# RWKV-7 and differential attention, one layer: dense products among the second head pair's transposes

## The chip, the cores and the metric

The kernel runs on one core of a Trainium2 chip. Five engines work beside each other, each on its own list of instructions: TensorE (matmuls, into PSUM), VectorE (DVE), ScalarE (ACT), GpSimd (POOL) and SyncE (SP, which issues most DMAs). The metric is the device time of one execution in microseconds (us), the median of several runs.

## The reference, cut to what matters

One decoder layer on 512 prompt tokens and 8 x 8 sample tokens, 576 columns in all, with a model width of 1024. Everything is float32.

```python
def layer_forward(x, prev_row, S0, attend, lam_init, lp):
    xn = rmsnorm(x, lp['g_mix'], NORM_EPS)
    P = xn @ lp['w_in']                        # RWKV columns, q k v, two gates
    ...
    Pr = Pr + (Pprev - Pr) * lp['mu_shift']    # token shift
    o_a, S = rwkv7_branch(Pr, S0, lp)          # 8 heads of 64, a recurrence over tokens
    ...
    att = attend(q, k, v, lam)                 # differential attention with ALiBi
    m = gate_a * (o_a @ lp['w_br_a']) + gate_b * (o_b @ lp['w_br_b'])
    x = x + m @ lp['w_out']
    hn = rmsnorm(x, lp['g_ffn'], NORM_EPS)
    x = x + jnp.square(jax.nn.relu(hn @ lp['w_up'])) @ lp['w_down']

def rwkv7_scan(S0, r, w, k, v, a, b):
    def step(S, inp):
        r_t, w_t, k_t, v_t, a_t, b_t = inp
        sa = jnp.einsum('bhij,bhj->bhi', S, a_t)
        S = S * w_t[:, :, None, :] + sa[..., None] * b_t[:, :, None, :] + v_t[..., None] * k_t[:, :, None, :]
        return S, jnp.einsum('bhij,bhj->bhi', S, r_t)
```

## The kernel before, in words

Activations lie transposed in SBUF, channels on the 128 partitions and 576 tokens along the free axis. Each weight matrix is streamed in blocks of 128 output channels. A block's weights are split in a high and a low half, and each 128 x 288 result is built from three products per 128 input channels: high by high, high by low, low by high. These are the **dense products**: `ps_z` (the RWKV projections, `shifted`), `ps_g` (the gates, `gate`), `ps_brb` and `ps_bra` (the two branch outputs), and later `ps_wo`, `u...` and `ps_dn` (output projection and MLP).

`stream` (a generator) yields before every product. Generators stand in a list, `waiting`. `take(n)` issues the next n products of that list at this place of the program; `fill(n)` does the same, and queues each of them behind the last matmul that the program has issued so far (`ring["mm"]`, set by the helpers `mm` and `tr`), by an edge that only fixes the order on TensorE. A planner turns the program into one order for each engine: of what it holds ready it takes what stands first in the program. So a taken product may be moved forward into any time in which it thinks that TensorE waits; a filled one not beyond its matmul. Each product adds to the bank of the one before, so products leave the list strictly in order. The kernel uses eight banks of PSUM: two for the dense products, three ("psw") that `bank` hands out in turn for most other work, three for the inverse and the chain.

The RWKV branch works on four **head pairs** (hp 0 to 3, two heads of 64 on 128 partitions). `rwkv(hp)` is a generator of stages, and `run(...)` advances it by one stage per number:

- A: key norms (`pn`), decay and rate (`pw`, `pa`), normalised keys (`pk`), bonus (`pbn`), then the masked 128 x 128 score blocks of nine chunks of tokens (`pA`), which VectorE masks out of PSUM into `ABR` and `ST`. Two groups of 8 products are asked for, behind pn and behind pa.
- B: token-major transposes of v (`pV`, five, evacuated by ScalarE into `SVU`) and of the keys (`pK`, nine, into `KBt`), the DMA of the sample states `s0`, and their products (`pI`).
- C: a triangular inverse by doubling (`pW`, `pZ`, eight blocks in turn, each with 9 products tied behind it, after one product by itself), ending in `TT`.
- D: new sample states (`pF`). E: mean and variance. F: transposes back (`pTy`), gate (`pg`), and the output `oa`, for hp 2 and 3 split into the halves `oab` that `ps_bra` reads.

`chain(pr)` is the recurrence over nine chunks for two head pairs at once (`pch`, `pY`).

The order is written out by hand at the end of this part of the kernel (lines 1051 to 1081): stages and numbers of products in turn. What the change touches: `run(0, 1, 1)` ran stage C of hp 0 and A and B of hp 1; `take(106)` came behind them, and `run(1)` was stage C of hp 1. In B of hp 1 eight products were asked for, with `take`, behind pK.

Of the kernel before, what the change touches and what calls it, by code (L numbers as in the profile page):

```python
# [41 lines left out]
def tile_hybrid_step(ctx, tc, xT, xsT, ktab, vtab, s0T, ptab, w_in, vecs, w2a2, g2, lamv,  # L42
# [14 lines left out]
    def act(out, in_, func=AF.Copy, **kw):  # L57
        ring["act"] = AE.activation(out=out, in_=in_, func=func, **kw)  # L58
# [9 lines left out]
    def ts(out, a, s1, op0, s2=None, op1=ALU.bypass, eng=None):  # L68
        (eng or VE).tensor_scalar(out=out, in0=a, scalar1=s1, scalar2=s2, op0=op0, op1=op1)

    def mm(out, lhsT, rhs, start=True, stop=True):
        ring["mm"] = PE.matmul(out=out, lhsT=lhsT, rhs=rhs, start=start, stop=stop)  # L72
        return ring["mm"]
# [27 lines left out]
    def bank(name):  # L101
        return psw.tile([P, 512], F32, tag="w", name=name)
# [113 lines left out]
    def take(n):  # L216

        while waiting and n:
            if next(waiting[0], None) is None:
                waiting.pop(0)  # L220
            else:
                n -= 1

    def fill(n):

        with tc.issue_after(ring["mm"].ins):
            take(n)
# [514 lines left out]
    def rwkv(hp):  # L742
# [11 lines left out]
        pn = bank(f"pn{hp}")  # L754
        for t, o in enumerate(toks):
            mm(pn[:, 2 * t:2 * t + 2], sq[:, o:o + P], c[:, C_HS:C_HS + 2])
        (fill if hp != 2 else take)(8)
        nr = stat.tile([P, 10], F32, tag="nr", name=f"nr{hp}")
        ts(nr, pn[:, 0:10], 1e-24, MAX)
        GE.tensor_tensor(out=nr, in0=nr, in1=mhalf[:, :10], op=ALU.pow)  # L760
# [6 lines left out]
        for t0, n in HALF:  # L767
# [3 lines left out]
            pa = bank(f"pa{hp}{t0}")  # L771
            mm(pa[:, :n], al[:, hs], Pt[12][:, t0:t0 + n])
            act(aa[:, t0:t0 + n], pa[:, :n], AF.Tanh, scale=0.5, bias=hw0[:, 4 + hp:5 + hp])
        (fill if hp != 2 else take)(8)
        ts(u, u, 1.0, ADD)
        cum = tmp("cum")
        VE.tensor_tensor_scan(out=cum, data0=reset, data1=u, initial=0.0, op0=MUL, op1=ADD)
# [65 lines left out]
        for cs, pV in two_chunks(f"pV{hp}", vv):  # L843
            for a, c0, c1 in cs:
                src = pV[64 * a:64 * a + 64].rearrange("p (c w) -> p c w", w=P)[:, :(c1 - c0 + 1) // 2]
                act(SVU[64:128, c0:c1:2, 0], src[:, :, 0:64])
                act(SVU[0:64, c0:c1:2, 1], src[:, :, 64:128])
        if hp >= 2:
            fill(8)
        KBt = rb_.tile([P, NCH, 2, 64], F32, tag="KBt", name=f"KBt{hp}")  # L850
        for c0, cn in ((0, 4), (4, 4), (8, 1)):
# [5 lines left out]

        s0 = rt.tile([P, NB, 64], F32, tag="s0", name=f"s0_{hp}")
        nc.sync.dma_start(out=s0, in_=s0T[hp])
        (fill if hp == 3 else take)(8)  # L860
        pI = bank(f"pI{hp}")
        for b in range(NB):
            for par, rows in halves:
# [177 lines left out]


    gens = [rwkv(hp) for hp in range(4)]

    def run(*stages):
        for hp in stages:
            while Pt[8 + hp] is None:
                take(2)
            next(gens[hp], None)
# [3 lines left out]
    waiting += ga[:5]  # L1053
    run(0, 0)
    take(221)
    run(0, 1, 1)
    take(106)
    run(1)
    chain(0)
    run(2, 0, 1)  # L1060
    take(190)
# [422 lines left out]
```

## Time and profile before

| | us |
|---|---|
| median of 3 runs | 1004.05 |
| lowest, highest | 1003.92, 1005.98 |
| the profiled execution | 1006.88 |
| its span, first to last instruction | 1005.1 |
| TensorE busy in it | 975.1 (97%) |
| VectorE busy | 688.9 (69%) |
| ScalarE busy | 497.0 (49%) |
| GpSimd busy | 87.5 (9%) |

A table by stretches gives busy time of each engine between two times from the span's start, and TensorE's granted clock as a share of full speed (1.00 is 2.4 GHz, 0.50 is 1.2 GHz). A timeline lists instructions in order of time; equal ones in a row are merged into one line. The number in brackets is idle time of the engine just before, and what ended it. "PE" is TensorE.

### The profile page before, as it was taken

Reading aid. Unit: us, or ns where it says so; the run is one execution under the profiler, and the core shown is the slowest. Engines: PE = TensorE matmul, PEld = TensorE weight load, DVE = VectorE, ACT = ScalarE, POOL = GpSimd, SP = SyncE. Lnnn points to the kernel's source line nnn. Section 1 sums busy time; section 2 is a strip of 40 time slices with the busy share of each in tenths; the row PEclk is TensorE's granted clock in tenths of the full one; section 3 lists DMA queues with packets and bytes.
Section 4 is the critical chain, followed back from the end, with each engine's and each line's share of the span. In section 5 each row is a group of like instructions: output and inputs, shape, how many; then the busy total and the mean of one; then the engine's idle time right before and its main releaser. Section 6 shows DMA issues by size and latency. Waiting matters only on the chain.

```text
span 1005.1 us, 24415 instructions
## 1 busy us (share of the span) xinstructions
PE 975.1 (97%) x10012; PEld 919.4 (91%) x10012; DVE 688.9 (69%) x1459; ACT 497.0 (49%) x1094; POOL 87.5 (9%) x171
## 2 busy tenths in 40 slices
PE   9999999899999998999989999999999999999996
PEld 9999998898887887988779999999999999999996
DVE  6698566864946679444579898966666666666644
ACT  6576455354435355453334666644444444444732
POOL 2511001301010340000210000000000000000001
PEclk9999999999989999999999999999999999999999
DMA  7422673211111234323357642222222222221402
GB/s 266 136 70 83 205 223 114 61 64 45 43 59 45 69 106 152 104 81 113 103 182 225 206 140 86 83 95 85 88 92 85 85 84 85 84 87 41 135 3 95
DMA packets 50833, 105.75 MB, mean 105 GB/s; under 512 B 6066, under 2 KB 8114, under 8 KB 50594
## 3 DMA queue, kind: packets, MB, share of 16 engines
q1 hardware_dynamic: 47442, 96.95, 30.4%
q0 software_dynamic: 1648, 5.35, 1.5%
q8 instruction: 79, 1.29, 0.5%
q10 hardware_dynamic: 1632, 1.89, 0.5%
q14 instruction: 32, 0.26, 0.1%
HBM read 89.38 MB, written 14.78 MB: 104 GB/s over the span
## 4 chain that ended last, share of the span: by engine, by line
PE 83%; DVE 6%; ACT 4%; issue 3%; DMA 2%; POOL 1%; SPq 0%; DVEq 0%; ACTq 0%; POOLq 0%
PE ps_dn L72 20%; PE ps_g L72 8%; PE ps_z L72 8%; PE ua L1220 5%; PE ux L1220 5%; PE ps_wo L72 4%; PE ps_k L72 3%; PE uc L1220 3%; PE ub L1220 3%; PE ud L1220 2%; PE ps_bra L72 2%; PE ps_q L72 2%; PE pch L72 2%; PE ps_brb L72 2%; PE ps_v L72 2%
## 5 line engine op out<-in xcount | busy, mean ns | idle before, releaser
L72 PE MATMUL ps_dn<-q,hi_dn 128*128 128x288 f32 x768 | 154.7, 296 | 0.0
L72 PEld LDWEIGHTS ps_dn<-q,hi_dn 128*128 128x128 f32 x768 | 122.7, 188 | 1.4
L72 PE MATMUL ps_dn<-q,lo_dn 128*128 128x288 f32 x384 | 113.2, 295 | 0.0
L72 PE MATMUL ps_g<-xl,hi_g 128*128 128x288 f32 x256 | 79.7, 311 | 0.0
L72 PE MATMUL ps_g<-xh,hi_g 128*128 128x288 f32 x256 | 79.0, 309 | 0.0
L72 PE MATMUL ps_g<-xh,lo_g 128*128 128x288 f32 x256 | 79.0, 309 | 0.0
L72 PEld LDWEIGHTS ps_dn<-q,lo_dn 128*128 128x128 f32 x384 | 72.0, 188 | 0.0
L72 PE MATMUL ps_z<-xh,lo_z 128*128 128x288 f32 (+1 forms) x224 | 68.9, 308 | 0.0
L72 PE MATMUL ps_z<-xh,hi_z 128*128 128x288 f32 (+1 forms) x224 | 67.6, 302 | 0.0
L72 PE MATMUL ps_z<-xl,hi_z 128*128 128x288 f32 (+1 forms) x224 | 66.8, 298 | 0.0
L61 DVE TENSOR_TENSOR ya<-ya,ps_dn 128x288 f32<-128x288 f32 x96 | 43.2, 451 | 29.4 <-PE ps_dn L72 29.4
L58 ACT ACTIVATE hi_dn<-raw_dn 128x512 fp32r<-128x512 f32 x48 | 30.1, 628 | 57.0 <-PE ps_dn L72 57.0
L1220 PE MATMUL ua<-h_b,hi 128*128 128x288 f32 x256 | 53.2, 298 | 0.0
L1220 PE MATMUL ux<-h_t,hi 128*128 128x288 f32 x256 | 52.3, 296 | 0.0
L58 ACT ACTIVATE c<-c 128x288 f32<-128x288 f32 x112 | 48.4, 439 | 7.4 <-DVE c L61 5.8
L72 PEld LDWEIGHTS ps_g<-xh,hi_g 128*128 128x128 f32 x256 | 48.7, 190 | 3.1 <-issue 1.8
L72 PEld LDWEIGHTS ps_g<-xl,hi_g 128*128 128x128 f32 x256 | 48.6, 190 | 1.9
L72 PEld LDWEIGHTS ps_g<-xh,lo_g 128*128 128x128 f32 x256 | 48.6, 190 | 1.6 <-DVE lo_g L61 0.2
L58 ACT ACTIVATE hi<-a 128x1024 fp32r<-128x1024 f32 (+1 forms) x32 | 27.1, 846 | 42.0 <-PE ps_dn L72 34.2
L72 PE MATMUL ps_dn<-q,w 128*128 128x320 f32 (+1 forms) x336 | 46.3, 297 | 0.0
L61 DVE TENSOR_TENSOR lo<-s,hi 128x1024 fp32r<-128x1024 f32 x32 | 39.2, 1224 | 10.1 <-ACT hi L58 10.0
L72 PEld LDWEIGHTS ps_dn<-q,w 128*128 128x128 f32 x336 | 45.3, 190 | 0.1
(395 smaller groups left out, 2802.2 us busy)
## 6 DMA issues: line engine op xcount, KB each, us to landing
a<-in_w_up_dram SPq DMA_DIRECT2D x32, 512.0 KB, 3.4
raw_dn<-in_w_down_dram SPq DMA_DIRECT2D x64, 256.0 KB, 2.8
raw_g<-in_w_in_dram SPq DMA_DIRECT2D x32, 256.0 KB, 3.1
raw_z<-in_w_in_dram SPq DMA_DIRECT2D x28, 256.0 KB, 3.1
gt_d<-gg SPq DMA_DIRECT2D x16, 288.0 KB, 2.4
g<-gt_d SPq DMA_DIRECT2D x16, 288.0 KB, 3.6
kp<-in_ktab_dram SPq DMA_DIRECT2D x16, 256.0 KB, 4.5
vp<-in_vtab_dram SPq DMA_DIRECT2D x16, 256.0 KB, 3.8
```

The lines of the kernel that those rows point to most:

```text
L58: ring["act"] = AE.activation(out=out, in_=in_, func=func, **kw)
L61: ins = (eng or VE).tensor_tensor(out=out, in0=a, in1=b, op=op)
L72: ring["mm"] = PE.matmul(out=out, lhsT=lhsT, rhs=rhs, start=start, stop=stop)
L1220: ring["mm"] = PE.matmul(out=ps[:, :288], lhsT=l[:, k], rhs=hb[blk][:, h, k], start=start and i == 0, stop=i == 11, skip_group_check=skip)
```

## The change

Stage B of hp 1 is now run behind the 106 products, directly ahead of its stage C. In that stage 8 products are asked for behind pV, which were not asked for before, and the 8 behind pK are now filled where they were taken. In stage A of hp 2 the two groups of 8 are filled where they were taken.

```diff
-        (fill if hp != 2 else take)(8)
+        fill(8)
         nr = stat.tile([P, 10], F32, tag="nr", name=f"nr{hp}")
...
-        (fill if hp != 2 else take)(8)
+        fill(8)
         ts(u, u, 1.0, ADD)
...
-        if hp >= 2:
+        if hp >= 1:
             fill(8)
         KBt = rb_.tile([P, NCH, 2, 64], F32, tag="KBt", name=f"KBt{hp}")
...
-        (fill if hp == 3 else take)(8)
+        (fill if hp in (1, 3) else take)(8)
         pI = bank(f"pI{hp}")
...
     run(0, 0)
     take(221)
-    run(0, 1, 1)
+    run(0, 1)
     take(106)
-    run(1)
+    run(1, 1)
     chain(0)
```

## Rows read from the trace of the kernel before

**Rows 1.** The page: the chain of work that ended last, shares of the span by engine.
```profile
PE 83%; DVE 6%; ACT 4%; issue 3%; DMA 2%; POOL 1%; SPq 0%; DVEq 0%; ACTq 0%; POOLq 0%
```

**Rows 2.** Table by stretches: length, busy us (instructions) per engine, PE's granted clock, DMA.
```profile
core 0: us, PE busy (x) PEld busy (x) DVE busy (x) ACT busy (x) POOL busy (x), PEclk, DMA share, GB/s
271.80:276.50 4.70, 3.46 (x60) 2.84 (x59) 3.81 (x11) 4.53 (x12) 0.00 (x0) 1.00 0.00 0
276.50:283.30 6.80, 6.80 (x103) 5.70 (x105) 2.62 (x7) 2.28 (x8) 2.67 (x2) 0.52 0.01 2
359.50:369.00 9.50, 8.72 (x88) 7.91 (x87) 5.34 (x13) 5.79 (x17) 1.89 (x1) 1.00 0.43 136
396.20:400.40 4.20, 3.64 (x100) 2.75 (x99) 3.29 (x9) 2.95 (x9) 0.00 (x0) 1.00 0.09 30
```

**Rows 3.** The same table for ps_z alone, ps_g alone, and ps_z in a full stretch.
```profile
241.50:272.70 31.20, 15.61 (x104) 14.19 (x103) 2.19 (x5) 1.00 0.18 52
...
241.50:272.70 31.20, 4.93 (x28) 3.90 (x28) 0.46 (x1) 1.00 0.18 52
...
249.70:259.90 10.20, 10.20 (x75) 10.04 (x75) 0.90 (x2) 1.00 0.15 53
```

**Rows 4.** Timeline of TensorE, stages B and C of hp 1: start, length, instruction.
```profile
272.64 0.33 PE L76 MATMUL pV<-cst_sb,P 128*128 128x128 f32 x1
273.40 1.20 PE L76 MATMUL pK<-cst_sb,KB 128*128 128x128 f32 x9 [0.43 <-ACT SVU L58]
275.41 1.11 PE L72 MATMUL pI<-ST,s 64*64 64x16 f32 x32 [0.81 <-ACT KBt L58]
276.45 2.05 PE L72 MATMUL pn<-cst_sb,sq 128*128 128x2 f32 x10
278.36 1.31 PE L72 MATMUL pw<-P,wl 128*128 128x288 f32 x2
279.60 1.19 PE L72 MATMUL pW<-X,DM 32*32 32x32 f32 x72
...
283.17 0.97 PE L72 MATMUL pZ<-W,Y 32*32 32x32 f32 x72
```

**Rows 5.** Timeline of TensorE: the same instructions at full clock.
```profile
242.06 1.28 PE L72 MATMUL pn<-cst_sb,sq 128*128 128x2 f32 x10
...
245.19 0.65 PE L72 MATMUL pw<-P,wl 128*128 128x288 f32 x2
...
285.46 0.82 PE L72 MATMUL pW<-X,DM 32*32 32x32 f32 x72
...
287.59 0.82 PE L72 MATMUL pZ<-W,Y 32*32 32x32 f32 x72
```

**Rows 6.** Timeline of VectorE, end of stage A and begin of C of hp 1.
```profile
271.64 0.67 DVE L61 TENSOR_TENSOR ST<-pA,cst_sb 64x512 f32<-64x512 f32 x1
...
276.25 0.47 DVE L884 STREAM_TRANSPOSE X<-Y 128x288 f32<-128x288 f32 x1
```

**Rows 7.** Timeline of TensorE, stage B of hp 2.
```profile
364.44 1.11 PE L72 MATMUL pI<-ST,s 64*64 64x16 f32 x32 [0.66 <-DMA s<-in_s0T_dram]
```

**Rows 8.** Timeline of SP's DMA issues (first to last of merged ones).
```profile
173.69 0.90 SPq L859 DMA_DIRECT2D s<-in_s0T_dram  x2
...
255.30 29.21 SPq L150 DMA_DIRECT2D raw_g<-in_w_in_dram  x5
```

**Rows 9.** Timeline, end of the RWKV stage: hp 3's output and the branch that reads it.
```profile
524.47 0.46 DVE L61 TENSOR_TENSOR oa<-oa,pg 128x288 f32<-128x288 f32 x1
...
524.86 0.63 ACT L58 ACTIVATE hi_bra<-raw_bra 128x512 fp32r<-128x512 f32 x1 [1.83 <-PE ps_brb L72]
...
525.39 1.00 ACT L58 ACTIVATE oab<-oa 128x288 fp32r<-128x288 f32 x2
...
527.67 0.40 PE L72 MATMUL ps_bra<-oab,hi_bra 128*128 128x288 f32 x1 [0.69 <-DVE oab L61]
```

**Rows 10.** Timeline: the last pa of hp 2; table by stretches, ps_g in one link of chain(0).
```profile
303.83 0.65 PE L72 MATMUL pa<-P,al 128*128 128x288 f32 x2
...
306.78:311.45 4.67, 2.43 (x15) 2.05 (x15) 0.44 (x1) 1.00 0.00 0
```

## The prediction

> **What bounds the kernel now.** I read the page's chain of waits first: TensorE carries 83% of what ended last, and no other engine more than 6% [rows 1]. So a change of order is worth what it takes out of TensorE's own time: stretches in which it waits, and stretches in which it runs at the lower clock. Next I looked in the table by stretches for both, around the code that is touched. The work of head pair 1 ends in such a place: in 271.80 to 276.50 TensorE is busy 3.46 us of 4.70, and right behind it, in 276.50 to 283.30, the granted clock is 0.52, its lower level of 1.2 GHz [rows 2]. The instructions of that place in order of time are [rows 4]: five transposes pV (the fifth at 272.64), nine pK after a wait of 0.43 us for ScalarE, 32 small products pI after a wait of 0.81 us, ten pn and two pw of head pair 2, and then pW, the first step of pair 1's triangular inverse. No dense product stands between the fifth pV and the end of pW.
>
> Why none stands there follows from the code and a count. Products leave the queue strictly in order, because each adds to the bank of the one before. Between the last product tied to pair 0's inverse and pair 1's inverse, the program before asks for 8 + 8 (in stage A), 8 (in B), 106 and 1, together 131. The rows of that stretch hold 104 ps_z and 28 ps_g [rows 3], 132, one of which began before it. So the budget is used up at 271.8: the planner spent nearly all of it while stage A waited for VectorE. The next product of the queue is tied behind pW, and everything behind it is closed as well.
>
> **The change part by part.**
>
> *The order of 106 and stage B.* The numbers asked for are the same. Pair 1's stage B, one DMA of s0 with it, is now behind the 106 in the program, though both are free to be issued when ready. The products cannot make stage A shorter: the banks for pV come free as VectorE finishes the masks of stage A, the last but one at 271.64 + 0.67 = 272.31 [rows 6], and pair 1's inverse needs X, which VectorE delivers at 276.25 + 0.47 = 276.72. The DMA of s0 was issued at 173.69 [rows 8], some 100 us ahead of its reader, before the queue of weights that it is moved past in the program; I cost it at nothing. If SP instead issued it late, pI would wait as pair 2's does, 0.66 us [rows 7]; a whole jam behind a waiting weight load is a rival below.
>
> *Sixteen products behind pV and pK instead of eight free ones.* Of the 131, 122 are now free or tied to early instructions, so the budget runs out eight products sooner, that is 8 x 0.136 = 1.09 us (75 products in 10.20 us [rows 3]) before 271.8; that time is lost to a wait, since the fifth pV cannot come before 272.31. Then eight stand behind it and eight behind pK, and one behind pI. At full clock the sequence from the end of the fifth pV (272.64 + 0.33 = 272.97) is: 1.09 for eight products, pK 1.20, 1.09 again, pI 1.11, one product 0.14, pn 1.28 and pw 0.65 (both at full clock in [rows 5]), less 0.28 by which these overlap in [rows 4] (0.07, 0.14 and 0.07), then 2.95 from the begin of pW to the end of pZ with nine products between (285.46 to 287.59 + 0.82, also [rows 5]). The end of pZ comes to 272.97 + 9.23 = 282.20. Before it was 283.17 + 0.97 = 284.14. Gain 1.9 us. In other words: the waits of 0.43 and 0.81 us get filled, 3.1 us of lower clock go (from 276.45 to 284.14 it took 7.69 us; 1.28 + 0.65 - 0.28 + 2.95 = 4.60 at full clock), and 16 x 0.136 = 2.2 us of products are paid there. Whether the filling alone is worth anything hangs on the clock. For its staying up speaks pair 2's same stage, with eight products behind pV, behind pK and behind pn: clock 1.00 [rows 2], although pI waited 0.66 us [rows 7]. So does 396.20 to 400.40, with no dense product in 4.20 us and TensorE busy 3.64: clock 1.00 [rows 2]. Against it: behind pI only one product comes before pn and pw, so pI, pn, pw and pW still stand together, 3.6 us. I take the clock as held, since the nearer row (the same stage of pair 2) held it.
>
> *take to fill in pair 2's stage A.* Sixteen products that were free are now behind the last pn and the last pa. Before, that pa was issued at 303.83 [rows 10], right after pair 1's inverse, and the chain over the chunks had begun only then. I cost it at nothing: pair 1's 73 tied products come first in the queue in any case, and TensorE has pa, pw and the chain's own products beside them. If that cover fails, the 190 behind are closed too; that is the slow rival.
>
> *The end of the stage.* Eight more products are spent early, so eight fewer are left after the second "take(47)". That would give 1.09 us back if TensorE were the limit there. It isn't: behind those products TensorE waits 0.69 us for VectorE's oab [rows 9], and oab hangs on ScalarE and VectorE, not on the products. One thing moves: ScalarE converts hi_bra (524.86, 0.63 us) as soon as the last of those products is done, and the oab behind it starts at 525.39 although its oa was ready at 524.47 + 0.46 = 524.93. With the conversion 1.09 us earlier that 0.4 us goes. Between 0 and 0.5, I take 0.4.
>
> *Sum.* 1.9 + 0.4 = 2.3 us less. The profiled execution took 1006.88 us, 1.8 of it around the span of 1005.1, so it would come to 1004.6. The median of the runs before is 1004.05, 2.8 lower than that execution, so I carry the difference over and forecast 1001.8. Bounds from the same rows: if all waits and all of the lower clock go and the products cost nothing because they fill time that is idle for VectorE anyway, 1.24 + 3.1 + 0.4 = 4.7 less, 999.3. If the lower clock stays as it was, 3.1 - 2.3 = 0.8 more, 1004.9.
>
> **A weight against the sum.** The profile shows one execution with 6.8 us at the lower clock here [rows 2]; the timed runs before spread over 1003.92 to 1005.98, and all lie below the profiled 1006.88. So the timed ones may lose less to the clock than the profiled one. The Trainium skill says the same in "TensorE: Matmul & The Clock Gate", Part 1: what watches the engine's activity runs free and does not start over with the kernel, so one kernel meets it at another point in another run. No run shown so far has a second clock record to test that. It makes the first rival.
>
> **The rivals.**
>
> 1. *The timed runs lose only half as much to the clock as the profile.* Then the change gains 2.3 - 1.55 = 0.75 us: 1003.3. For it: the 2.8 us between profile and median. Against it: an execution with a profile may be slower for other reasons.
> 2. *The clock falls all the same,* for pI, pn, pw and pW still stand together: 0.8 us more, 1004.9. For it: the second half of the lower-clock stretch was pn and pw. Against it: 396.20 to 400.40 [rows 2].
> 3. *Slower: pair 2's ties close the queue during chain(0).* A link of that chain lasts 4.67 us and takes 15 products, 2.0 us, to fill its waits (306.78 to 311.45 [rows 10]). If the last pa is put off behind k links, because the banks go to the chain and stage A's transposes first, k x 2.0 us of waits stay open. It decides from the third link: 6.1 - 2.3 = 3.8 more, 1007.9. For it: pn ran at 276.45 but this pa only at 303.83, so it is put off already. Against it: eight products before and eight behind pa are the order that the trace shows anyway.
> 4. *The lower clock begins earlier and lasts.* With eight products fewer before the fifth pV the clock falls there, and the sixteen run at 0.264 instead of 0.136 (nine products between pW and pZ: 283.17 - 280.79 = 2.38 us [rows 4]): 16 x 0.128 = 2.05, with 3.1 for the rest and 1.2 if pK doubles, less 2.3: 4.0 more, 1008.1.
> 5. *s0 goes behind a waiting weight load.* Five issues of weights are spread over 255.30 to 284.51 [rows 8], the last of them held until a buffer is free; behind that one pI would come some nine microseconds late: 1011.
>
> **How the numbers follow.** Forecast 0.55, rivals 0.12, 0.12, 0.15, 0.04 and 0.02. A measurement of this kernel tells a difference from 0.2%, 2.0 us; the forecast sits close to that bound. Of its 0.55 I count 0.41 past it, since a planner that has products in reach may also fill the small waits nearby, up to 999.3, and 0.14 short of it. With rivals 1 and 2 "same" gets 0.38, and rivals 3 to 5 give "slower" 0.21. The range goes from the lower bound, 999.3, to 1006.3, which takes in rivals 1 and 2 and two links of rival 3 (4.1 - 2.3 = 1.8 more, 1005.9). The forecast's own range is 999.3 to 1003.0.
>
> **What would show it.** In the profile after: eight products each between the fifth pV and pK and between pK and pI, and one behind pI; no wait over 0.2 us of pK or pI for ScalarE; no granted clock under 1.0 between 270 and 285; the first pZ of pair 1 ending near 282; the last pa of pair 2 within 5 us of the end of pair 1's inverse; some nine products, not 17, behind the last "take(47)", with a longer wait for oab. The prediction is wrong if the clock falls in that stretch again, if the fifth pV is early enough for the time lost before it to be no loss, or if waits open in chain(0).

## Result: 1.0022 of before, slower, and where the gain of the stage went

The changed kernel takes 1007.02 us (median of 22 runs), the one before 1005.41 in the same set: ratio 1.0022, interval 1.0013 to 1.0031. The forecast was 1001.8. That is 0.2% slower, with the whole interval above 1. The profiled execution took 1007.12 us with a span of 1005.3; the profiled one before took 1006.88 with 1005.1, so the two profiles stand closer to each other than the medians do.

The page after, the chain that ended last; it answers to [rows 1]:

```profile
PE 82%; DVE 7%; ACT 4%; issue 3%; DMA 2%; POOL 2%; SPq 0%; DVEq 0%; POOLq 0%; ACTq 0%
```

VectorE and GpSimd hold a per cent more of that chain each, TensorE one less. The views below show which of their work that is. First the place that was changed, table by stretches (columns as in [rows 2]) and TensorE's timeline, after:

```profile
272.70:277.60 4.90, 4.77 (x61) 4.47 (x60) 4.12 (x12) 4.73 (x13) 0.00 (x0) 1.00 0.02 3
277.60:281.70 4.10, 4.10 (x165) 3.84 (x164) 1.76 (x5) 0.95 (x5) 2.36 (x2) 1.00 0.22 68
```
```profile
272.75 0.33 PE L76 MATMUL pV<-cst_sb,P 128*128 128x128 f32 x1
...
273.98 1.15 PE L76 MATMUL pK<-cst_sb,KB 128*128 128x128 f32 x9
...
276.33 1.11 PE L72 MATMUL pI<-ST,s 64*64 64x16 f32 x32
...
277.61 1.17 PE L72 MATMUL pn<-cst_sb,sq 128*128 128x2 f32 x10
278.70 0.82 PE L72 MATMUL pW<-X,DM 32*32 32x32 f32 x72
...
280.85 0.82 PE L72 MATMUL pZ<-W,Y 32*32 32x32 f32 x72
```

This is the stage as forecast: eight products in each of the first two gaps, one behind pI, no wait of any size, clock 1.00. The first pZ ends at 280.85 + 0.82 = 281.67, before at 284.14 [rows 4], and pWc, at the end of pair 1's inverse, starts 2.2 us sooner. Pair 2's two pw, which stood ahead of pW before, are no longer there. TensorE's timeline before, then after:

```profile
299.15 0.69 PE L72 MATMUL pWc<-X,ABR 32*32 32x32 f32 x32
```
```profile
296.96 0.69 PE L72 MATMUL pWc<-X,ABR 32*32 32x32 f32 x32
```

What is won there is lost later, and the next two views show where. Table by stretches of ps_g alone, from pWc to pair 2's first pA (chain(0)), and from there to pair 2's first pV (stage A); behind the length stand TensorE's matmuls and its weight loads. Before, then after:

```profile
299.15:343.90 44.75, 26.12 (x144) 19.99 (x143) 2.75 (x7) 1.00 0.17 56
343.90:359.60 15.70, 9.66 (x65) 8.54 (x63) 0.91 (x2) 1.00 0.27 93
```
```profile
296.96:343.61 46.65, 28.02 (x153) 21.18 (x152) 2.72 (x6) 1.00 0.19 63
343.61:360.73 17.12, 8.28 (x54) 7.35 (x54) 0.97 (x3) 1.00 0.13 39
```

By the weight loads, 143 products in chain(0) became 152, and 63 in stage A became 54: nine moved from stage A into chain(0), and the two pw came into chain(0) from the other side, from pair 1's stage. Chain(0) takes 1.9 us more for that. But stage A, with nine products less, takes 1.4 us more, not less. Timelines of GpSimd, VectorE and TensorE there, before and then after:

```profile
342.05 3.27 POOL L818 MEMSET ST<- 64x1152 f32 x3
...
345.29 0.75 DVE L61 TENSOR_TENSOR ST<-P,pe 64x576 f32<-64x576 f32 x1
345.41 3.55 POOL L61 TENSOR_TENSOR vm<-SVU,cst_sb 128x512 f32<-128x512 f32 x3
```
```profile
341.80 2.17 POOL L818 MEMSET ST<- 64x1152 f32 x2
...
343.73 3.88 DVE L61 TENSOR_TENSOR ST<-P,pe 64x576 f32<-64x576 f32 x1
343.95 3.04 POOL L61 TENSOR_TENSOR vm<-SVU,cst_sb 128x512 f32<-128x512 f32 x3
...
349.85 1.13 PE L72 MATMUL pA<-ST,KB 128*128 128x128 f32 x8 [2.34 <-DVE ST L61]
```

The same VectorE instruction, the last ST of pair 2, took 0.75 us before and 3.88 after. Through that time GpSimd runs three vm (the masked values for pairs 0 and 1, stage D); pair 2's score products pA wait 2.34 us behind ST. In the order before, a third memset stood ahead of the vm on GpSimd, the first vm came 0.12 us behind ST, and it was the vm that took longer (1.54 us against 1.04). The Trainium skill has a mechanism for this in "SBUF — State Buffer", section "SBUF: two separate sides": a VectorE instruction with two inputs in SBUF and a GpSimd instruction that reads SBUF contend for one pair of ports; the one that starts first holds it for its whole instruction, and the other one waits. The rows agree that one waits for the other (3.88 against 0.75 us). On which one waits they differ: here ST's record starts 0.22 us ahead of the first vm (343.73 against 343.95), and it still waits for all three. No run here looks at the ports themselves.

The lower clock did go from pair 1's stage, but it shows at pair 2's stage B, where pn, pw and pa stand together. Table by stretches, after:

```profile
366.00:369.10 3.10, 3.08 (x49) 3.07 (x50) 0.27 (x2) 1.34 (x5) 0.41 (x1) 1.00 0.31 109
369.10:372.60 3.50, 3.50 (x11) 2.64 (x10) 2.32 (x4) 2.04 (x5) 3.33 (x3) 0.51 0.33 122
```

### The profile page after: what moved, and what is told of

Same layout as the page of the kernel before. It is cut to its first block, busy times and chain, and to the rows that moved or that the text cites. A ratio compares the mean times of both kernels' runs of the same rounds, so it can differ in the third digit from the quotient of the medians.

```text
span 1005.3 us, 24413 instructions
## 1 busy us (share of the span) xinstructions
PE 971.7 (97%) x10012; PEld 916.8 (91%) x10012; DVE 692.0 (69%) x1459; ACT 497.5 (49%) x1094; POOL 87.6 (9%) x171
## 3 DMA queue, kind: packets, MB, share of 16 engines
q8 instruction: 79, 1.29, 0.5%
## 4 chain that ended last, share of the span: by engine, by line
PE 82%; DVE 7%; ACT 4%; issue 3%; DMA 2%; POOL 2%; SPq 0%; DVEq 0%; POOLq 0%; ACTq 0%
PE ps_dn L72 20%; PE ps_g L72 8%; PE ps_z L72 8%; PE ua L1220 5%; PE ux L1220 5%; PE ps_wo L72 4%; PE ps_k L72 3%; PE uc L1220 3%; PE ub L1220 3%; PE ps_bra L72 2%; PE ud L1220 2%; PE pch L72 2%; PE ps_q L72 2%; PE ps_v L72 2%; PE ps_brb L72 2%
```

## Experiments

Theory A: the collision of ST with vm costs the loss. Theory B: the nine products and the two pw moved into chain(0) cost it. Theory C: it is the place of the lower clock. All ratios are to the kernel before, run beside it on the same chip; e9 to e12 ran on another chip than the other experiments.

**The changed kernel again** (e1, no edit).

> The changed kernel itself once more, for a second profile. Theory A (a collision): VectorE's last ST<-P,pe of head pair 2 (two operands in SBUF) meets GpSimd's three vm there; it lasted 3.88 us instead of 0.75, and TensorE then waited 2.34 us for pA, which takes back what stage C of head pair 1 won (2.2 us). Then this profile shows that op over 3 us again and the ratio is near 1.002. Theory B (order alone): pA waits 2 us or more even where that op takes 0.75 us, since the nine products that stood there are now in chain(0). Theory C (the clock alone): the op and the wait vary, and the slower runs are those with a lower granted clock.

1.0027 (1.0015 to 1.0039); the ST took 3.86 us. The collision is no accident of one execution.

**The two halves alone** (e2: the order of 106 and stage B, products taken; e3: the fills, order as before).

```diff
-    run(0, 1, 1)
+    run(0, 1)
     take(106)
-    run(1)
+    run(1, 1)
```
```diff
-        if hp >= 2:
+        if hp >= 1:
             fill(8)
...
-        (fill if hp == 3 else take)(8)
+        (fill if hp in (1, 3) else take)(8)
```

> Only stage B of head pair 1 is moved behind the 106; its eight products stay free and none is asked for behind pV. The budget up to pI stays 131, so the stretch behind the fifth pV stays bare: by theories A, B and C alike no gain there, the clock falls near 276 as before, the end of the first pZ within 1 us of 284.1, the time within 0.1% of before. If the move by itself is what disturbs the later stages, it is slower by 1 to 2 us.

> Only the fills: eight products behind pV and eight behind pK, with stage B of head pair 1 still ahead of the 106. Products leave the queue in order, so the 106 are closed until pK is issued and stage A of head pair 1 waits bare for VectorE, about 10 us (75 + 34 products stood there before). Expected 6 to 10 us slower than before, with the clock low around 252 to 270; if the products make up for it later in full, no slower.

e2: 1.0039 (1.0024 to 1.0053), 3.9 us and so a miss: the expectation was 0.1%, or 1 to 2 us if the move disturbs later stages. The local gain isn't there (0.50 is granted in 276.90 to 283.70, and pair 1's pWc comes 1.2 us later than before), and the move alone reorders what stands behind. From pWc to pair 2's first pV it takes 62.4 us where it took 60.4. Both ST of pair 2 meet the vm, in a milder form; pA's wait for that is 0.63 us, and the rest of the loss isn't explained. GpSimd, VectorE and TensorE:

```profile
346.88 4.14 POOL L61 TENSOR_TENSOR vm<-SVU,cst_sb 128x512 f32<-128x512 f32 x3
347.11 1.49 DVE L66 SCALAR_TENSOR_TENSOR ST<-sq,u 64x576 f32<-64x576 f32 x1
...
348.52 1.60 DVE L61 TENSOR_TENSOR ST<-P,pe 64x576 f32<-64x576 f32 x1
...
351.70 0.46 PE L72 MATMUL pA<-ST,KB 128*128 128x128 f32 x2 [0.63 <-DVE ST L61]
```

e3: 1.0149 (1.0130 to 1.0169), some 13 to 15 us where 6 to 10 were expected. As expected, the 106 are closed behind pK, stage A of pair 1 is bare, and TensorE idles at the lower clock:

```profile
251.80:265.50 13.70, 7.17 (x27) 6.12 (x28) 11.74 (x20) 2.23 (x3) 0.10 (x1) 0.50 0.00 1
```

From pair 1's first pn to pWc that costs 7.0 us (64.1 against 57.1). Behind it the collision is there as well: pair 2's last ST takes 3.88 us, and pA waits 2.35. So neither half is a gain by itself, and both parts of the change are needed for its local gain.

**vm late** (e4: the vm of pairs 0 and 1 wait for the last mask of pair 2's stage A).

```diff
+        masked[hp] = ring["tt"]
...
+            if hp < 2:
+                tc.add_manual_dep(vi.ins, masked[2].ins.name, ...)
```

> The changed kernel with one wait added: GpSimd's vm of head pairs 0 and 1 wait for the last mask of head pair 2's stage A, so they cannot meet ST<-P,pe. Theory A: that op takes 0.75 us, no wait of pA over 0.5 us, and the kernel is 2 to 3 us faster than the changed one, about 0.1% faster than before or better. Theory B: pA still waits about 2 us and the time stays at 1.002. Theory C: the time stays, with the clock as before.

1.0011 (1.0002 to 1.0021), 1.6 us less than e1, not 2 to 3: the ST is at 0.75 again and pA's wait is gone, but the vm now come so late that pF waits for them (0.65 us and three times 0.15), and three other VectorE instructions beside them take longer, two of them shown here (0.84 and 1.29 us; the same two take 0.45 before):

```profile
354.17 4.69 POOL L935 TENSOR_TENSOR vm<-SVU,cst_sb 128x512 f32<-128x512 f32 x4 [7.53 <-DVE ST L61]
354.68 0.84 DVE L61 TENSOR_TENSOR Y<-DT,cst_sb 128x288 f32<-128x288 f32 x1
...
355.44 1.29 DVE L61 TENSOR_TENSOR DM<-DT,cst_sb 128x288 f32<-128x288 f32 x1
```

**As many products ahead as before** (e5, and e12 the same).

```diff
-    take(106)
+    take(98)
```

> The changed kernel with take(98) in place of take(106), so that as many products stand ahead of pair 1's inverse as before the change, and from there on the order of TensorE is that of before: 143 dense products, not 152, between pair 1's last pW and pair 2's first pA, and pair 2's pw ahead of that pW. Theory B, the nine products and the pw moved into the chain over the chunks cost the loss: the local gain of some 1 to 2 us stays, chain(0) falls from 46.6 to 44.8 us, and the kernel is 2 us faster than the changed one, as fast as before or 1 us faster (0.999 to 1.000). Theory A, the collision of VectorE's ST with GpSimd's vm costs the loss: if the ST of pair 2's stage A falls behind the vm again, pA waits over 2 us again and the kernel stays at 1.002; if the order of before brings it back ahead of the vm, it cannot be told from B by the time, but by this row. Theory C, the place of the lower clock decides: the time follows the granted clock alone, and it is 1.002 wherever the lower clock falls at pair 2's stage B.

> The version with take(98) once more, beside the others of this set: 0.997 to 1.000 of before; a second profile shows whether the lower clock stays off pair 1's stages B and C there.

0.9983 (0.9970 to 0.9996) and 0.9986 (0.9975 to 0.9996): the local gain, kept. Chain(0) is back at 44.77 us, stage A at 15.68. GpSimd's order is that of before and the ST takes 0.75, so A and B aren't told apart yet. Granted clock: 1.00 in e5 between 273.30 and 281.80, 0.72 in e12's 278.50 to 284.00.

**No vm on GpSimd** (e6 on the changed kernel, e7 on the one before).

```diff
-               c[:, C_MB:C_MB + NB]..., MUL, GE)
+               c[:, C_MB:C_MB + NB]..., MUL, GE if hp >= 2 else None)
```

> The changed kernel with the four vm of pairs 0 and 1 on VectorE in place of GpSimd, so that no instruction of GpSimd holds the port pair there. Theory A: the ST takes 0.75 us and not 3.88, pA's wait of 2.34 us goes, 1.5 to 3 us less than the changed kernel if VectorE's own four vm (some 0.6 us each, an estimate by its other operations with two inputs) find room, net 0.998 to 1.001 of before. Theory B: no gain, 1.002 to 1.004, since the nine products and the pw are still in the chain and VectorE has 2.4 us more to do. Theory C: no gain, as long as the clock falls at pair 2's stage B.

> The control of the run before: the kernel before the change with the same four vm on VectorE. Where the ST takes 0.75 us already nothing is to be gained. Theory A: 0 to 2 us slower than before (1.000 to 1.002), so the edit is worth 2 us or more better in the changed kernel than here. Theories B and C: the edit has the same effect on both kernels, whatever it is.

e6 0.9992 (0.9978 to 1.0005), e7 0.9988 (0.9975 to 1.0000): with no vm on GpSimd the times can't tell the two orders apart. In e6 the ST takes 0.75 us and pA doesn't wait. The edit is worth 3.5 us on the changed kernel (1.0027 to 0.9992) and 1.2 on the one before. That A expected no gain on the latter was a miss. Stage A is 2.1 us longer there (17.76) without a wait of TensorE: the pF of the two heads come one after the other, 1.07 us each, four times, where before two heads together took 1.08 and 1.39. But pair 3's stages, which come in another order, are shorter by more (391.38 to 415.19 from its first pA to its first pI, 23.8 us, against 27.9).

In e6 the lower clock stands where it stood in the changed kernel, at pair 2's stage B (0.72 granted in 366.00 to 372.00). So Theory C, which had the time stay at 1.002 with the lower clock there, doesn't hold.

**The kernel before again** (e8).

> The kernel before the change once more, for a second profile. If the stretch of lower clock behind pair 1's stage B (6.83 us from 276.75) belongs to the order of the work, it stands at the same place in a second execution; if it is left to chance, it stands elsewhere or is gone. Ratio 1.000.

1.0007 (0.9993 to 1.0022). The lower clock stands at the same place (0.51 granted in 277.60 to 284.40), and from pair 1's first pn to pWc it takes 57.2 us (57.1 in the first profile). In e7, whose order is the same up to there, 0.76 was granted between 276 and 283, and the stretch took 55.6: the loss to the clock isn't the same in each execution, as the forecast's first rival supposed for the timed runs.

**The best of both** (e9: take(98), and the vm on VectorE).

> Both edits that helped, on the changed kernel: take(98) in place of take(106), and the four vm of pairs 0 and 1 on VectorE. With take(98) the ST already takes 0.75 us, so theory A has nothing left for the vm to give; but the same edit was worth 1.5 us on the kernel before, where the ST took 0.75 us too (the first vm took 1.54 rather than 1.04 us there, and pF may follow). If the two add: 1002.4 - 1.5 = about 1001, 0.997 of before. If not: 0.998.

0.9961 (0.9946 to 0.9976): by the ratios the two add. It is faster than the kernel before and the changed one.

**Only GpSimd's order** (e10 on take(98): pair 3's memset waits for pair 2's last mask, so the vm come first; e11 on the changed kernel: the vm wait for pair 2's second ST, so the memset comes first). By their profiles the order of TensorE is left as it is in each. The first edit is e10's, the second e11's.

```diff
+            if hp == 3:
+                tc.add_manual_dep(zero.ins, masked[2].ins.name, ...)
```
```diff
             tt(st[rows, :, 1], ch(r)[rows], ch(pe)[rows], MUL)
+            masked[hp] = ring["tt"]
...
+            if hp < 2:
+                tc.add_manual_dep(vi.ins, masked[2].ins.name, ...)
```

> The version with take(98), whose only edit is GpSimd's order: the memset of pair 3's ST, which stood ahead of the vm, waits for pair 2's last mask, so that the vm start about a microsecond earlier, before pair 2's ST. TensorE's order is the same. Theory A: the ST of 0.75 us takes over 3 us, pA waits some 2 us, and the kernel is some 2 us slower than with take(98) alone: 1.000 of before. Theory B: as fast as with take(98) alone, 0.998, since the products stand where they stood.

> The mirror of it: the changed kernel, whose only edit is that the vm of pairs 0 and 1 wait for pair 2's second ST; GpSimd then does the memset of pair 3's ST first, as in the kernel before, and TensorE's order is that of the changed kernel. Theory A: the ST takes 0.75 us, pA's wait of 2.34 us goes, and about 2.3 us of the changed kernel's time: 1.0000 to 1.0005 of before. Theory B: 1.002 to 1.003, as the changed kernel. What is left over 0.998, the time with take(98), is then the price of the nine products and the two pw moved into chain(0).

e10 1.0006 (0.9995 to 1.0018), where take(98) alone is 0.9986 beside it; e11 0.9982 (0.9970 to 0.9995), where the changed kernel was 1.0027 on the other chip. Both moved the way that A said, with all products where they stood. In e11 the ST takes 0.75 us and pA doesn't wait. But e10's collision is smaller than A said: ST gets through behind the first vm and takes 1.61 us, pA waits 0.24.

```profile
343.21 3.57 POOL L61 TENSOR_TENSOR vm<-SVU,cst_sb 128x512 f32<-128x512 f32 x3
343.26 1.61 DVE L61 TENSOR_TENSOR ST<-P,pe 64x576 f32<-64x576 f32 x1
...
346.46 1.13 PE L72 MATMUL pA<-ST,KB 128*128 128x128 f32 x8 [0.24 <-DVE ST L61]
```

Stage A is only 0.5 us longer (16.20), so most of e10's 2 us lies elsewhere: pair 3's first pA to its first pI takes 28.7 us against 27.5 in e12, for a reason that no run shows. e10 alone doesn't show A.

**The collision sized on one chip** (e13 the changed kernel, e14 as e11, e15 the same edit on the kernel before, e16 on take(98)).

> The changed kernel once more, on the same chip as the next three: 1.002 to 1.003 of before, the ST near 3.9 us.

> Its twin, GpSimd's vm behind pair 2's second ST and all else the same. By the rows alone the collision is worth 2.65 us (56.76 against 54.11 us from pair 1's last pW to pair 2's first pF), so theory A expects 0.9973 to 0.9980 of the changed kernel on the same chip. If the difference is 4 us or more again (0.996), a part of it lies outside that stretch, and the clock or the small issue gaps in pair 3's stages would have to show it.

> The same edit on the kernel before, where GpSimd's memset already stands ahead of the vm; here the edit also puts the second memset of pair 3 ahead, so the vm come a microsecond later. Theory A: nothing to take away but the half microsecond that the first vm waits: 0.999 to 1.001 of before. If it gains as much as in the changed kernel (0.996 of its own), the edit helps for another reason than the collision.

> The same edit on the version with take(98). Theory A: as fast as take(98) alone, 0.998 to 0.999 of before. Beside the second run it shows what the nine products and the two pw in chain(0) cost once nothing collides: by the rows 0.7 us (61.12 against 60.45 us from pair 1's last pW to pair 2's fifth pV), too little to tell from the times.

e13 1.0028 (1.0016 to 1.0039), e14 0.9990 (0.9978 to 1.0001), e15 1.0001 (0.9992 to 1.0010), e16 0.9994 (0.9984 to 1.0003). The edit takes 3.8 us from the changed kernel and nothing from the one before. For take(98), 0.9994 lies above the 0.998 to 0.999 that was expected and above e5 and e12, with intervals that overlap. By the profiles e13 and e14 issue the same instructions in the same order on TensorE, VectorE and ScalarE; on GpSimd one memset of ST stands ahead of the vm in e14 and behind them in e13. The collision is gone in e14:

```profile
343.84 0.75 DVE L61 TENSOR_TENSOR ST<-P,pe 64x576 f32<-64x576 f32 x1
345.28 3.05 POOL L935 TENSOR_TENSOR vm<-SVU,cst_sb 128x512 f32<-128x512 f32 x3
```

Table by stretches from pWc to the first pF of pair 0's stage D, e13 and then e14:

```profile
297.82:354.58 56.76, 54.27 (x626) 45.21 (x626) 38.27 (x91) 25.65 (x65) 9.23 (x13) 1.00 0.15 52
```
```profile
297.05:351.17 54.12, 53.97 (x627) 45.19 (x626) 35.20 (x91) 25.77 (x65) 9.20 (x13) 1.00 0.16 55
```

VectorE is busy 3.07 us less, TensorE waits 2.49 - 0.15 = 2.34 us less, and the stretch is 2.64 us shorter. The ratios say 0.0038; with intervals of 0.0012 to either side on both, that is some 2.2 to 5.4 us, so the rows' 2.64 lies within. The rest can be the clock: the mean granted clock of the timed runs is 0.9907 in e13 and 0.9928 in e14, and among the runs of either kernel 0.001 less goes with 0.6 us more, so an estimate from these numbers gives 1.2 us. Whether the collision costs that clock or chance does isn't shown (the 22 runs of the changed kernel in the first set had 0.9928 too). The lower clock at pair 2's stage B isn't it: in e14 it lasts longer (0.51 granted in 365.00 to 372.00) and the loss is gone all the same. The nine products and the two pw by themselves: pWc to pair 2's first pV is 61.13 us in e14 and 60.46 in e16, 0.7 us, which the times can't tell (0.9990 and 0.9994).

## Why the prediction was wrong

**The local step was right.** Forecast: the first pZ ends at 282.20; it ended at 281.67. The half microsecond more is no gain: the sum had pair 2's two pw (0.65 us) ahead of pW, and they went into chain(0). The clock held there in the changed kernel's profile and in e1. It doesn't always, so that it held in both is in part luck: e13 has 0.69 in 279.00 to 284.50 (and loses nothing by it: 54.6 us from pair 1's first pn to pWc, as without), e6 and e14 have 0.72 in 278.00 to 284.00, and e12 has 0.72 (56.2 us). And the gain depends on what the order before loses there: 57.1 - 54.7 = 2.4 us by the two profiles, 55.6 - 54.7 = 0.9 by e7's. Take(98), which keeps the rest as before, measures it at 1.4 to 1.7 us in e5 and e12, and e16 at 0.6. The timed runs bear out the clock's part: with take(98) their mean granted clock is 0.9944, 0.9937 and 0.9936, where the kernel before had 0.9921, 0.9922 and 0.9921 beside it.

**Pair 2's fills at nothing, and s0 at nothing: right.** Pair 2's last pa starts at 302.64, before at 303.83 [rows 10], and s0 is issued at 173.80, before at 173.69 [rows 8]. Take(98) has the same fills, and its chain(0) and stage A are as long as before. The rivals of a closed chain(0) and of a late s0 fall. Timelines of TensorE and SP, after:

```profile
302.64 0.75 PE L72 MATMUL pa<-P,al 128*128 128x288 f32 x2
```
```profile
173.80 0.90 SPq L859 DMA_DIRECT2D s<-in_s0T_dram  x2
```

**The step that failed is "The end of the stage", and with it the sum 1.9 + 0.4, which puts everything between pair 1's inverse and that end at nothing.** It had the eight products, spent early, missing only behind the second "take(47)". They were not missing there: 17 still stand behind the last pTy, and hi_bra and oab come at the same distance as in [rows 9], so the 0.4 us didn't come:

```profile
524.93 0.63 ACT L58 ACTIVATE hi_bra<-raw_bra 128x512 fp32r<-128x512 f32 x1 [1.83 <-PE ps_brb L72]
525.47 1.00 ACT L58 ACTIVATE oab<-oa 128x288 fp32r<-128x288 f32 x2
```
```profile
527.75 0.40 PE L72 MATMUL ps_bra<-oab,hi_bra 128*128 128x288 f32 x1 [0.69 <-DVE oab L61]
```

They were missing 80 us earlier. Until `run(3)` has passed, the list holds nothing but projections and gates, and it runs out behind the last pZ of pair 3's inverse: two products stand there, and nine before (the eighth came in chain(1) before). ps_g from that pZ to pair 3's pWc, before and then after:

```profile
439.05:441.12 2.07, 1.46 (x10) 1.22 (x9) 0.00 (x0) 1.00 0.03 8
440.22:441.70 1.48, 0.61 (x3) 0.30 (x2) 0.22 (x1) 1.00 0.59 169
```

Nothing is won by that: from this pWc to the first pF of pairs 2 and 3 it takes 58.2 us after and 57.5 before.

From pair 1's inverse to that place the order ran eight products ahead, so what stood in each stage shifted. Chain(0) took nine more, stage A nine fewer. With the two pw, that alone costs 0.7 us. What decided is that the planner then also put GpSimd's instructions in another order, and the vm met VectorE's ST: 2.64 us. With the local gain, -2.4 + 0.7 + 2.64 = 0.9 us slower, and 2.4 where the order before loses less to the clock; measured were 1.6 by the medians and 2.2 by the ratio. The two profiles agree with this as far as the first pF of pairs 2 and 3, which comes 1.2 us later. Behind it the profiled execution before loses about as much to a lower clock of its own (0.57 granted in 512.20 to 516.20, after 1.00), so their spans end 0.2 us apart. No rival held this. The slow rivals looked at TensorE's products and SP's queue, none at two engines that hold a few per cent of the chain of waits each and get in each other's way.

**The size carried over.** The profiled execution before stood 1.5 to 2.8 us above the medians, and the forecast took 2.3 us from it as a whole. Part of that gain was a loss to the clock that not every run has in full: of the four profiles with the order of before in this place, three have 6.8 us of lower clock there (the first, e8, e15) and e7 has half of it. Over the whole execution the timed runs of before lose no less than the profiled one: their mean granted clock is 0.992 (beside e1, e5, e9 and e13), and the profiled execution had 0.993. Where in the execution they lose it isn't on record, so what lifted the profiled time above the medians stays open.

## What to carry over

When free work is spent earlier, everything behind it in a strict queue moves: follow the shift through each later stage, not only to its end. A planner that reorders one engine may reorder the others too, so before trusting a local gain, look in the later stages for pairs of VectorE and GpSimd instructions that both read SBUF and stand within a fraction of a microsecond of each other, and ask what waits behind the VectorE one. Two versions that differ only in one engine's order (here e13 and e14) size such a collision without moving anything else.

## What the runs showed of the hardware that was not expected

VectorE's ST was held up not by one but by three GpSimd instructions in a row (3.88, 3.86 and 3.88 us in three profiles of the changed kernel, 3.88 in e3), although by the records it starts 0.2 us ahead of the first vm. With the vm 0.12 us behind ST, it was the vm that gave way (ST 0.75 us, vm 1.54, in both profiles of before and both of take(98)). In e10 ST was held up by one vm only (1.61 us). Which of them goes first isn't explained by the recorded starts. Where the vm met no ST it took 1.04 us.
